# Layer 0's attention inputs projected with features on partitions, and queries and keys reloaded in thirds

## The chip, the cores and the metric

The kernel runs on one core of one Trainium2 chip. The metric is the device time of one execution in microseconds. The kernel before took 3854.85 us, the median of 3 runs (3852.91 to 3861.53).

## The reference

One step of a two-layer model: 128 context tokens and 1024 latent tokens (a grid 64 wide), 1152 tokens of 1024 features, fp32. The change concerns the attention of layer 0. Its input projection gives for every token queries, keys and values of 8 neighbourhood heads of 64 features and of 4 differential heads, whose queries and keys have two parts of 64 and whose values have 128:

```python
nq, nk, nv, dq, dk, dv = attn_projections(h_lat, w_in_attn[i])
dq, dk = axial_rope(dq), axial_rope(dk)          # per half of 32: [x1*cos - x2*sin, x1*sin + x2*cos]
o_na = neighbourhood_attention(nq, nk, nv, cache_na_k[:, i], cache_na_v[:, i], na_rpb[i])
k_all = jnp.concatenate([dk, cache_diff_k[:, i]], axis=1)
v_all = jnp.concatenate([dv, cache_diff_v[:, i]], axis=1)
o_df = diff_attention(dq, k_all, v_all, lam, lam_init)
mix_lat = jnp.concatenate([...o_na..., ...o_df...], axis=-1) @ w_out_attn[i]
```

The context tokens go through the same projections without rotation, and attend to themselves alone; their keys and values are outputs too. Differential attention takes two softmaxes (one of each part of queries and keys), subtracts lam times the second from the first, multiplies with the values and normalises. Neighbourhood attention lets a latent token see a window of 8 rows by 16 columns, with a bias, and the 128 cached tokens.

## The kernel before, in words

Products of fp32 numbers are made from a high and a low part (fp32r), three matmuls for one. Activations h and weights are split in that way, and for the scores the high and low parts of 64 features are stacked to 128 rows, so that two matmuls make one product.

*Projection.* `attn_in` (L355) with `proj_tok` (L332) works in 8 groups g: 0 to 3 are the differential heads, 4 to 7 pairs of neighbourhood heads. A group's weights are 8 blocks of 128 features by 384 columns (queries, keys, values, 128 each), loaded (L338) and split. For each of 9 tiles of 128 tokens, 24 matmuls with the tile's activations stationary and 384 weight columns streaming (L350 to L352) give tokens on partitions; ScalarE copies the result (L368, tile `ist`) and a write (L369) puts it into the DRAM tensor `qkv[g]`.

*Keys of a head.* `prep_k` (L408) loads them back in three pieces (L417 to L422, `kraw`). `stage` (L381) rotates the differential ones (VectorE L387 and L394, GpSimd L397) and splits them (ScalarE L403 or L405, VectorE L406). 20 turns on TensorE by the identity (L429) put features on partitions, and ScalarE copies them into the tile `K` (L434, L437).

*Queries.* For each of a head's 9 units (a unit is a head and 128 query tokens) `prep_q` (L440) does the same with one tile (`qraw`, L504 or L617; the neighbourhood gather L617 takes 8 x 16 rows of the grid): 4 turns (L446) and a cast into `Q` by VectorE (L448).

*Units.* `pipe` (L567) runs units with lags of their steps between them: preparing `Q`, scores (L518, L519; L636, L645), exponentials (L524), turning the probabilities (L476) and multiplying with the values (L482). Between the steps `fill` pulls background work: in stage A, the differential heads, 0.28 of a projection step of the later groups and 0.3 of a step of the adaptive vectors (`aw` loads L128, sums L181); in stage B, the neighbourhood heads, the output projection (weights `owraw`, L744, one buffer; attention results `xr`, L699 and L702). Stage B also loads the biases (`nab`, L624, two for each unit) and values (`vw`, on GpSimd's queue).

*Order.* The source gives the steps, and a scheduler with a timeline of its own sets the order of the instructions on each engine and on SP, the queue that issues nearly all loads and writes. Tiles of one tag share a small number of buffers (`ist` 2, `qraw` 2, `kraw` 2, `K` 2, `Q` 3, `aw` 2), and an instruction that needs a buffer waits for its last readers. An engine, and SP, works in its order.

Of the kernel before, what the change touches and what calls it, by code (L numbers as in the profile page):

```python
# [40 lines left out]

SHARED = ("K", "Q", "pT", "qraw", "kraw", "st2", "st3", "mx", "sm")


class Net:
# [286 lines left out]
    def proj_tok(self, hH, hL, wsrc, ncol, pool, sink):  # L332

        nc = self.nc
        WH, WL = [], []
        for k in range(KT):
            raw = self.t(pool, [P, ncol], tag="wraw")
            nc.sync.dma_start(raw if ncol != GW else raw.rearrange("p (m c) -> p m c", c=P), wsrc(k))  # L338
            wh = self.t(pool, [P, ncol], F32R, tag="wh")
            wl = self.t(pool, [P, ncol], F32R, tag="wl")  # L340
            self.split(wh, wl, raw)
            WH.append(wh)
            WL.append(wl)
        yield
        for T in range(NT):
            pt = self.t(self.nps, [P, 512], tag="mm")
            c = slice(T * P, (T + 1) * P)
            for k in range(KT):
                mm = nc.tensor.matmul
                mm(pt[:, :ncol], lhsT=hH[k][:, c], rhs=WH[k], start=k == 0, stop=False)  # L350
                mm(pt[:, :ncol], lhsT=hH[k][:, c], rhs=WL[k], start=False, stop=False)  # L351
                mm(pt[:, :ncol], lhsT=hL[k][:, c], rhs=WH[k], start=False, stop=k == KT - 1)  # L352
            sink(T, pt)
            yield


    def attn_in(self, g, hH, hL, pool):
        nc, I, O = self.nc, self.I, self.O
        j = g if g < 4 else g - 4
        blk = 3 if g < 4 else 0  # L360
        w = I["w_in_attn"][0]

        def wsrc(k):
            return w[k * P : (k + 1) * P, :].rearrange("p (m c) -> p m c", c=512)[:, blk : blk + 3, j * P : (j + 1) * P]

        def sink(T, pt):
            st = self.t(pool, [P, GW], tag="ist")
            nc.scalar.copy(st, pt[:, :GW])  # L368
            nc.sync.dma_start(self.qkv[g][T * P : (T + 1) * P, :], st)  # L369
            if T == 0:  # L370
                if g < 4:
                    nc.scalar.dma_start(O[4][0, 0, :, j].rearrange("t c d -> t (c d)"), st[:, P : 2 * P])
                    nc.scalar.dma_start(O[5][0, 0, :, j], st[:, 2 * P :])
                else:
                    nc.scalar.dma_start(O[2][0, 0, :, 2 * j : 2 * j + 2].rearrange("t c d -> t (c d)"), st[:, P : 2 * P])
                    nc.scalar.dma_start(O[3][0, 0, :, 2 * j : 2 * j + 2].rearrange("t c d -> t (c d)"), st[:, 2 * P :])

        return self.proj_tok(hH, hL, wsrc, GW, pool, sink)

    def stage(self, p, raw, n, slots, scale, rope):  # L380

        nc = self.nc
        if rope is not None:
            cs, sn = rope
            m1 = self.t(p, [P, n, P], tag="rm1", bufs=1)
            m2 = self.t(p, [P, n, P], tag="rm2", bufs=1)
            nc.vector.tensor_tensor(  # L387
                m1.rearrange("p n (c d) -> p n c d", d=64),
                raw.rearrange("p n (c d) -> p n c d", d=64),
                cs.unsqueeze(2).to_broadcast([P, n, 2, 64]),  # L390
                op=ALU.mult,
            )
            sw = raw.rearrange("p n (h x q) -> p (n h) x q", x=2, q=16)[:, :, ::-1, :]
            nc.vector.tensor_tensor(  # L394
                m2.rearrange("p n (h x q) -> p (n h) x q", x=2, q=16), sw, sn.rearrange("p n (h x q) -> p (n h) x q", x=2, q=16), op=ALU.mult
            )
            nc.gpsimd.tensor_tensor(m1, m1, m2, op=ALU.add)  # L397
# [8 lines left out]
        nc.vector.scalar_tensor_tensor(st[:, :, 1, :], rv, scale, st[:, :, 0, :], op0=ALU.mult, op1=ALU.subtract)  # L406
        return st.rearrange("p a b c -> p a (b c)").bitcast(F32)

    def prep_k(self, g, cache, rope, p, ps):
        nc = self.nc  # L410
        K = self.t(p, [P, 2, 10 * P], F32R, tag="K")
        src = self.qkv[g]
        for tiles in ((0, 9), (1, 2, 3, 4), (5, 6, 7, 8)):
            n = len(tiles)
            raw = self.t(p, [P, n, P], tag="kraw")
            if tiles[0] == 0:
                nc.sync.dma_start(raw[:, 0, :], src[0:P, P : 2 * P])  # L417
                nc.sync.dma_start(raw[:, 1, :], cache)
# [1846 lines left out]
```

## Time and profile before

| | us |
|---|---|
| median of 3 runs | 3854.85 (3852.91 to 3861.53) |
| the profiled execution | 3851.15 |
| its span, first to last instruction | 3849.4 |
| stage A, projections and differential heads | 108 to 600 |
| boundary | 600 to 640 |
| stage B, neighbourhood heads | 640 to 911 |

The stage marks were read from the timeline. The rest of the span (layer 0's feed-forward, layer 1 and the normalisations) uses none of the changed functions. How to read the views: a group's row gives line, engine, operation, tile names (out<-in), shape and count, then busy us, mean ns of one, and the idle time just before, with what ended it. A window's row gives start and end, length, busy us (and instructions) of TensorE (PE), its weight loads (PEld), VectorE (DVE), ScalarE (ACT) and GpSimd (POOL), TensorE's granted clock, the mean busy share of the 16 DMA engines, and GB/s. A row of SP's timeline gives the start and length of the issue of a DMA, not of its transfer.

### The profile page before, as it was taken

How to read it: one execution, taken by the hardware profiler on the slowest of the kernel's cores; microseconds unless marked ns; L12 is line 12 of the kernel's file. 1: busy time of each engine (PE TensorE's matmuls, PEld its weight loads, DVE VectorE, ACT ScalarE, POOL GpSimd, SP SyncE). 2: the span in 40 equal slices, each digit the busy share in tenths (PEclk: the TensorE clock that was granted, in tenths of full speed). 3: DMA queues.
4: the chain of work that ended last, by engine and by line, in shares of the span. 5: the costliest groups of instructions: out<-in, count | busy, mean ns of one | idle time of the engine just before them, and what ended most of it. 6: DMA issues, size and time to landing. Idle time of an engine off the chain costs nothing.

```text
span 3849.4 us, 67037 instructions
## 1 busy us (share of the span) xinstructions
PE 3661.5 (95%) x24885; PEld 3444.4 (89%) x24885; DVE 2272.7 (59%) x5106; ACT 1404.6 (36%) x3361; POOL 1100.4 (29%) x1450
## 2 busy tenths in 40 slices
PE   7999997999999999999999998999998999999998
PEld 4899996999899999999989886877777899999998
DVE  6677864665945556665244556766665774444434
ACT  3445444555333333225332333233322533334221
POOL 2000002112222224333011323665662322324430
PEclk9999997999999999999999998999999999999999
DMA  6433325542223334442334336232223212223321
GB/s 209 125 94 107 113 69 133 133 109 61 64 85 108 91 99 143 149 137 86 106 105 130 115 129 212 58 88 65 65 60 108 62 60 75 75 73 107 116 88 61
DMA packets 425399, 392.16 MB, mean 102 GB/s; under 512 B 68172, under 2 KB 370376, under 8 KB 423536
## 3 DMA queue, kind: packets, MB, share of 16 engines
q1 hardware_dynamic: 406640, 376.29, 32.3%
q10 hardware_dynamic: 13152, 7.27, 0.7%
q0 software_dynamic: 5280, 4.31, 0.6%
q8 instruction: 197, 3.23, 0.3%
q14 instruction: 130, 1.06, 0.1%
HBM read 289.32 MB, written 98.33 MB: 101 GB/s over the span
## 4 chain that ended last, share of the span: by engine, by line
PE 74%; DVE 8%; DMA 8%; POOL 3%; issue 2%; ACT 2%; SPq 0%; DVEq 0%; ACTq 0%; POOLq 0%
PE mm L82 8%; PE mm L84 8%; PE mm L83 8%; PE A L1726 3%; PE A L1724 3%; PE A L1725 3%; PE o L482 3%; DMA aw<-in_w_ada_dram 2%; PE E L1724 2%; PE E L1725 2%; PE mm L350 2%; PE E L1726 2%; PE mm L352 2%; PE mm L351 2%; DVE aacc L181 2%
## 5 line engine op out<-in xcount | busy, mean ns | idle before, releaser
L729 DVE SCALAR_TENSOR_TENSOR x<-mm,mod,x 128x128 f32<-128x128 f32 (+1 forms) x576 | 277.2, 512 | 238.7 <-PE mm L84 237.9
L1636 POOL TENSOR_TENSOR wl<-raw,wh 128x512 fp32r<-128x512 f32 x120 | 167.1, 1392 | 567.2 <-ACT wh L1635 541.3
L1635 ACT CAST wh<-raw 128x512 fp32r<-128x512 f32 x288 | 178.3, 620 | 306.4 <-PE A L1725 107.4
L181 DVE SCALAR_TENSOR_TENSOR aacc<-aw,v,aacc 128x512 f32<-128x512 f32 x280 | 228.7, 849 | 75.2 <-DMA aw<-in_w_ada_dram 74.7
L350 PE MATMUL mm<-wh,hH 128*128 128x384 f32 x576 | 200.8, 349 | 11.5 <-ACT wh L74 4.7
L352 PE MATMUL mm<-wh,hL 128*128 128x384 f32 x576 | 195.8, 341 | 4.6 <-DVE hL L261 4.6
L351 PE MATMUL mm<-wl,hH 128*128 128x384 f32 x576 | 197.3, 342 | 1.0 <-DVE wl L75 0.9
L82 PE MATMUL mm<-hH,wh 128*128 128x384 f32 x528 | 184.6, 351 | 2.6 <-ACT wh L74 2.6
L84 PE MATMUL mm<-hH,wl 128*128 128x384 f32 x528 | 180.3, 344 | 3.4 <-DVE rst L867 2.1
L83 PE MATMUL mm<-hL,wh 128*128 128x384 f32 x528 | 180.3, 342 | 0.0
L1636 DVE TENSOR_TENSOR wl<-raw,wh 128x512 fp32r<-128x512 f32 x168 | 118.8, 708 | 102.1 <-ACT wh L1635 98.3
L397 POOL TENSOR_TENSOR rm<-rm,rm 128x128 f32<-128x128 f32 (+1 forms) x40 | 27.0, 676 | 461.2 <-DVE rm L387 329.0
L75 DVE TENSOR_TENSOR wl<-wraw,wh 128x256 fp32r<-128x256 f32 (+1 forms) x184 | 90.1, 508 | 108.3 <-ACT wh L74 78.7
L1150 PE MATMUL A<-AR,BK 64*128 64x256 f32 x576 | 116.8, 418 | 31.3 <-DVE KK L1154 18.6
L524 ACT ACTIVATE P<-S,mx 128x384 f32<-128x384 f32 (+1 forms) x200 | 112.2, 570 | 88.8 <-DVE mx L522 86.6
L82 PE MATMUL mm<-mh,owh 128*128 128x384 f32 x384 | 138.5, 375 | 5.2 <-ACT owh L74 2.7
L83 PE MATMUL mm<-ml,owh 128*128 128x384 f32 x384 | 132.5, 345 | 0.0
L84 PE MATMUL mm<-mh,owl 128*128 128x384 f32 x384 | 131.3, 342 | 1.2 <-DVE owl L75 1.2
L350 PEld LDWEIGHTS mm<-wh,hH 128*128 128x128 f32 x576 | 110.2, 191 | 16.2 <-ACT ist L368 7.7
L817 PE MATMUL mm<-wh,hH 128*128 128x256 f32 x432 | 124.0, 290 | 0.0
L1150 PEld LDWEIGHTS A<-AR,BK 64*128 64x128 f32 x576 | 75.4, 194 | 53.1 <-issue 20.0
L818 PE MATMUL mm<-wl,hH 128*128 128x256 f32 x432 | 122.4, 285 | 0.0
(540 smaller groups left out, 12501.5 us busy)
## 6 DMA issues: line engine op xcount, KB each, us to landing
raw<-in_w_ffn_in_dram SPq DMA_DIRECT2D x176, 256.0 KB
aw<-in_w_ada_dram SPq DMA_DIRECT2D x160, 256.0 KB
raw<-hdr SPq DMA_DIRECT2D x132, 192.0 KB
hdr<-c SPq DMA_DIRECT2D x160, 144.0 KB
raw<-in_w_ffn_out_dram SPq DMA_DIRECT2D x88, 256.0 KB
F<-stg SPq DMA_DIRECT2D x34, 640.0 KB
stg<-st SPq DMA_DIRECT2D x12, 1536.0 KB
qkv<-ist SPq DMA_DIRECT2D x72, 192.0 KB
```

What stands on the lines that cost most here:

```text
L82: mm(out, lhsT=wh, rhs=xh, start=first, stop=False)
L83: mm(out, lhsT=wh, rhs=xl, start=False, stop=False)
L84: mm(out, lhsT=wl, rhs=xh, start=False, stop=last)
L181: nc.vector.scalar_tensor_tensor(acc[:, c, :], w[:, 0, :], s, acc[:, c, :], op0=ALU.mult, op1=ALU.add)
L350: mm(pt[:, :ncol], lhsT=hH[k][:, c], rhs=WH[k], start=k == 0, stop=False)
L351: mm(pt[:, :ncol], lhsT=hH[k][:, c], rhs=WL[k], start=False, stop=False)
L352: mm(pt[:, :ncol], lhsT=hL[k][:, c], rhs=WH[k], start=False, stop=k == KT - 1)
L729: self.nc.vector.scalar_tensor_tensor(x[f][:, c], pt[:, a:b], self.mod[l][jg][:, f, cd : cd + 1], x[f][:, c], op0=ALU.mult, op1=ALU.add)
L1636: eng.tensor_tensor(wl, w, wh, op=ALU.subtract)
L1724: mm(o, lhsT=wh[:, ks], rhs=xh, start=new and k == 0, stop=False, skip_group_check=True)
L1725: mm(o, lhsT=wh[:, ks], rhs=xl, start=False, stop=False, skip_group_check=True)
L1726: mm(o, lhsT=wl[:, ks], rhs=xh, start=False, stop=k == 3, skip_group_check=True)
```

## The change

The projection takes the three parts of a group one after the other: keys, values, queries. Now a block of 128 weight columns is stationary and 384 tokens stream (`mm3`, L82 to L84): 9 steps of 24 matmuls as before, but the result has features on partitions. Keys and queries go to DRAM as `qf[g][m]`, 128 features x 1152 tokens. The differential heads' go a second time, as `qs[g][m]`, with neighbouring blocks of 16 features exchanged (8 writes of 16 rows), which is the partner that the rotation needs. Values are turned back to tokens on partitions by 3 turns for each third (L358), go to `vt[g]`. The context's keys for the output take one turn. Neighbourhood queries are written patch by patch, so that a unit's 128 tokens are together.

`heads_steps` prepares a head in 13 steps: the cached keys (2 turns, as they come by tokens), 6 pieces of keys and 6 of queries. A piece (`fm_piece`) is 64 features of one part by 384 tokens, loaded twice, onto partitions 0 to 63 and 64 to 127, by one DMA whose source pattern is 2 x 64 x 384, with a step of 0 in the 2 (`fraw`; in the built program the pattern is the same). For the rotation, the same pattern of `qs` (`fsw`), two products and a sum. Then ScalarE casts the high part for all rows, and VectorE subtracts: for keys on the lower 64 rows alone, for queries into a second tile. The units use slices of `K` and `Q`, with no turn. Steps of a head are pulled by `heads_hook` at the start of its units, and the first 9 of the next head's during the last four units; so the first neighbourhood head's begin in stage A. `ist` has 3 buffers, `fraw` 2, `fsw` 2.

SP at the start of the first head (group 0 just projected; `kraw` keys, `qraw` queries, `wraw` the next group's weights). Before:

```order
L417 DMA kraw_884<-qkv_107 128x128
L418 DMA kraw_884<-in_cache_diff_k_dram 128x128
L369 DMA qkv_107<-ist_768 128x384
L504 DMA qraw_946<-qkv_107 128x128
L504 DMA qraw_1048<-qkv_107 128x128
L369 DMA qkv_107<-ist_796 128x384
L422 DMA kraw_897<-qkv_107 128x4x128
L504 DMA qraw_1156<-qkv_107 128x128
L369 DMA qkv_107<-ist_824 128x384
L369 DMA qkv_107<-ist_852 128x384
L338 DMA wraw_990<-in_w_in_attn_dram 128x3x128
```
And now:

```order
L435 DMA kraw_981<-in_cache_diff_k_dram 128x128
L418 DMA fraw_990<-qf_108 128x1x384
L422 DMA fsw_992<-qs_124 128x1x256
L364 DMA vt_131<-ist_859 128x3x128
L418 DMA fraw_999<-qf_108 128x1x384
L422 DMA fsw_1001<-qs_124 128x1x256
L435 DMA kraw_1804<-in_cache_diff_k_dram 128x128
L422 DMA fsw_1010<-qs_124 128x1x384
L382 DMA qf_107<-ist_887 128x384
L386 DMA qs_123<-ist_887 16x384 x8
L364 DMA vt_131<-ist_902 128x3x128
L382 DMA qf_107<-ist_930 128x384
```
Loads of `qkv` tiles among the last writes of group 0 became pieces of keys, in a swapped and an unswapped copy; the writes of the queries and of their swapped copies (`qs_123`, eight each) stand behind the first of them, and the next weights further on.

TensorE in the middle of stage A, between projection matmuls (`T` a turn's result, `S` scores). Before:

```order
L351 MATMUL mm_1425<-wl_1005,hH_28_132 128x384
L476 MATMUL T_1260<-ident_60,P_1179 128x128 x4
L446 MATMUL T_1306<-ident_60,st_269_1302 128x128 x4
L352 MATMUL mm_1425<-wh_1004,hL_36_140 128x384
L350 MATMUL mm_1425<-wh_1010,hH_29_133 128x384
L351 MATMUL mm_1425<-wl_1011,hH_29_133 128x384
L352 MATMUL mm_1425<-wh_1010,hL_37_141 128x384
L518 MATMUL S_1390<-K_883,Q_1172 128x384
```
And now, at a like place:

```order
L83 MATMUL mm_1462<-hL_37_165,wh_1116 128x384
L84 MATMUL mm_1462<-hH_29_157,wl_1117 128x384
L502 MATMUL T_1385<-ident_60,P_1295 128x128 x4
L358 MATMUL T_1419<-ident_60,ist_1340 128x128 x3
L539 MATMUL S_1510<-K_980,Q_1044 128x384
L540 MATMUL S_1510<-K_980,Q_1044 128x384
```
The four turns of queries (L446) are gone; three turns of values by L358 stand at some of these places, and the scores' stationary operand is a slice of a query tile made for three units.

SP at the boundary between the stages (`owraw` output-projection weights, `xr` attention results and inputs, `nab` biases). Before:

```order
L702 DMA xr_7007<-in_x_sample_dram 128x3x128
L744 DMA owraw_7832<-in_w_out_attn_dram 128x1024
L744 DMA owraw_7939<-in_w_out_attn_dram 128x1024
L744 DMA owraw_8987<-in_w_out_attn_dram 128x1024
L744 DMA owraw_9111<-in_w_out_attn_dram 128x1024
L744 DMA owraw_10297<-in_w_out_attn_dram 128x1024
L624 DMA nab_1556_6878<-rpbd 128x1x384
L624 DMA nab_1557_6879<-rpbd 128x1x384
L624 DMA nab_1558_6880<-rpbd 128x1x384
L417 DMA kraw_7636<-qkv_112 128x128
L418 DMA kraw_7636<-in_cache_na_k_dram 128x128
L422 DMA kraw_7649<-qkv_112 128x4x128
```
And now:

```order
L761 DMA owraw_7730<-in_w_out_attn_dram 128x1024
L761 DMA owraw_7828<-in_w_out_attn_dram 128x1024
L418 DMA fraw_7272<-qf_118 128x1x384
L418 DMA fraw_7354<-qf_118 128x1x384
L761 DMA owraw_8769<-in_w_out_attn_dram 128x1024
L716 DMA xr_7025<-in_x_prompt_dram 128x128
L719 DMA xr_7025<-in_x_sample_dram 128x2x128
L418 DMA fraw_7358<-qf_118 128x1x384
L418 DMA fraw_7433<-qf_118 128x1x384
L761 DMA owraw_8875<-in_w_out_attn_dram 128x1024
L418 DMA fraw_7437<-qf_118 128x1x384
L418 DMA fraw_7519<-qf_118 128x1x384
```
The loads of output-projection weights, in a row before, have key pieces of the second pair of neighbourhood heads (`qf_118`) between them, and the first biases stand further on.

The diff, cut to its core:

```diff
     def attn_in(self, g, hH, hL, pool):
...
+        def turn(st, tg, n, dst):
+            pt = self.t(self.nps, [P, 512], tag="T")
+            for i in range(n):
+                nc.tensor.transpose(pt[:, i * P : (i + 1) * P], st[:, i * P : (i + 1) * P], self.ident)
+            o = self.t(pool, [P, GW], tag="ist")[:, : n * P]
+            nc.scalar.copy(o, pt[:, : n * P])
...
+        for m in (1, 2, 0):
+            ms = slice(m * P, (m + 1) * P)
+            for tg in range(TG):
+                sl = slice(tg * GW, (tg + 1) * GW)
+                pt = self.t(self.nps, [P, 512], tag="mm")
+                for k in range(KT):
+                    self.mm3(pt[:, :GW], WH[k][:, ms], WL[k][:, ms], hH[k][:, sl], hL[k][:, sl], k == 0, k == KT - 1)
+                st = self.t(pool, [P, GW], tag="ist")
...
+                        nc.sync.dma_start(self.qf[g][m][:, sl], st)
+                        if g < 4:
+                            for b in range(8):
+                                o = (b ^ 1) * 16
+                                nc.sync.dma_start(self.qs[g][m][o : o + 16, sl], st[b * 16 : b * 16 + 16])
...
+    def fm_piece(self, p, g, m, c, a, n, rope):
+        nc = self.nc
+        dup = lambda src, a, n: dap(src, 64 * c * TOK + a, [[0, 2], [TOK, 64], [1, n]])
+        raw = self.t(p, [P, GW], tag="fraw")[:, :n]
+        nc.sync.dma_start(raw, dup(self.qf[g][m], a, n))
+        if rope:
+            l0 = max(a, P) - a
+            sw = self.t(p, [P, GW], tag="fsw")[:, : n - l0]
+            nc.sync.dma_start(sw, dup(self.qs[g][m], a + l0, n - l0))
+            ts = slice(a + l0 - P, a + n - P)
+            nc.vector.tensor_tensor(sw, sw, self.sin[:, ts], op=ALU.mult)
+            nc.vector.tensor_tensor(raw[:, l0:], raw[:, l0:], self.cos[:, ts], op=ALU.mult)
+            nc.gpsimd.tensor_tensor(raw[:, l0:], raw[:, l0:], sw, op=ALU.add)
+        return raw
+
+    def heads_steps(self, g, cache, rope, scale, p, ps, head):
...
+        for tg in range(TG):
+            for c in range(2):
+                a = tg * GW
+                r = self.fm_piece(p, g, 1, c, a, GW, rope)
+                o = K[:, c, a : a + GW]
+                nc.scalar.copy(o, r)
+                nc.vector.tensor_tensor(o[64:], r[64:], o[64:], op=ALU.subtract)
+                yield
+        for tg in range(TG):
+            Q = head["Q", tg] = self.t(p, [P, 2, 2, GW], F32R, tag="Q")
+            for c in range(2):
+                r = self.fm_piece(p, g, 0, c, tg * GW, GW, rope)
+                nc.scalar.activation(Q[:, c, 0, :], r, AF.Copy, scale=scale)
+                nc.vector.scalar_tensor_tensor(Q[:, c, 1, :], r, scale, Q[:, c, 0, :], op0=ALU.mult, op1=ALU.subtract)
+                yield
+
+    def heads_hook(self, j, T, heads, gen):
...
+        upto(j, min(9 + T, 13))
+        if T >= 5 and j < 7:
+            upto(j + 1, (2, 4, 6, 9)[T - 5])
...
-            K, Q = head[j][0], st["Q"]
+            K, Q = head[j]["K"], head[j]["Q", T // 3][:, :, :, T % 3 * P : T % 3 * P + P]
...
-                nc.tensor.matmul(S[:, :ch], lhsT=Q[:, 2 * c, :], rhs=kk, start=True, stop=False)
+                nc.tensor.matmul(S[:, :ch], lhsT=Q[:, c, 0, :], rhs=kk, start=True, stop=False)
...
-                self.wpool = _Bufs(wp, {"wraw": 3, "wh": 9, "wl": 9, "ist": 2, "aw": 2})
+                self.wpool = _Bufs(wp, {"wraw": 3, "wh": 9, "wl": 9, "ist": 3, "aw": 2})
```

More of the change, by code (lines that the diff above doesn't have):

```diff
@@ L39, in dap @@
     return bass.AP(tensor=ap.tensor, offset=ap.offset + offset, ap=dims)
-SHARED = ("K", "Q", "pT", "qraw", "kraw", "st2", "st3", "mx", "sm")
+SHARED = ("K", "Q", "pT", "fraw", "kraw", "st", "mx", "sm")
 class Net:
@@ new lines, in heads_steps @@
+    def heads_steps(self, g, cache, rope, scale, p, ps, head):
+        nc = self.nc
+        K = head["K"] = self.t(p, [P, 2, 10 * P], F32R, tag="K")
+        raw = self.t(p, [P, P], tag="kraw")
+        nc.sync.dma_start(raw, cache)
+        st = self.t(p, [P, 2, 2, 64], F32R, tag="st")
+        rv = raw.rearrange("p (c d) -> p c d", d=64)
+        nc.scalar.copy(st[:, :, 0, :], rv)
+        nc.vector.tensor_tensor(st[:, :, 1, :], rv, st[:, :, 0, :], op=ALU.subtract)
+        sf = st.rearrange("p a b c -> p a (b c)").bitcast(F32)
+        yield
@@ L443, in prep_q @@
         pt = self.t(ps, [P, 512], tag="T")
         for c in range(2):
-            for s in range(2):
-                nc.tensor.transpose(pt[:, (c * 2 + s) * P : (c * 2 + s + 1) * P], st[:, c, s * 64 : s * 64 + P], self.ident)
-        Q = self.t(p, [P, 4, P], F32R, tag="Q")
-        nc.vector.tensor_copy(Q.rearrange("p a b -> p (a b)"), pt)
-        return Q
+            nc.tensor.transpose(pt[:, c * P : (c + 1) * P], sf[:, c, :], self.ident)
+        nc.scalar.copy(K[:, :, 9 * P :], pt[:, : 2 * P].rearrange("p (c t) -> p c t", c=2))
@@ L451, in diff_lam, with upto @@
+    def heads_hook(self, j, T, heads, gen):
+        def upto(j, k):
+            if j not in heads:
+                heads[j] = {"n": 0}
+                heads[j]["gen"] = gen(j, heads[j])
+            while heads[j]["n"] < k:
+                heads[j]["n"] += 1
+                next(heads[j]["gen"], None)
+        upto(j, min(9 + T, 13))
+        if T >= 5 and j < 7:
+            upto(j + 1, (2, 4, 6, 9)[T - 5])
     def diff_lam(self):
@@ L502, in a @@
         def a():
-            raw = self.t(p, [P, 1, P], tag="qraw")
-            nc.sync.dma_start(raw[:, 0, :], self.qkv[j][T * P : (T + 1) * P, 0:P])
-            st["Q"] = self.prep_q(p, ps, raw, None if T == 0 else (self.cos[:, T - 1 : T, :], self.sin[:, T - 1 : T, :]))
+            if T == 0:
+                head[j]["ob"] = self.t(p, [P, NT, P], tag="ob"), self.t(p, [P, NT], tag="oss", bufs=2)
         nk, k0, ch = (1, 0, P) if T == 0 else (9, P, GW)
@@ L1979, in attn @@
         wpool = self.wpool
+        done = set()
         def group(g):
-            return self.attn_in(g, hH, hL, wpool)
+            yield from self.first if g == 0 else self.attn_in(g, hH, hL, wpool)
+            done.add(g)
         due = {}
```

254 lines of the change are left out of this document (102 added, 152 removed).

## The prediction

> **What bounds the kernel now.** I read the page first: which engine is busiest, and what ends last.
>
> ```profile
> span 3849.4 us, 67037 instructions
> PE 3661.5 (95%) x24885; PEld 3444.4 (89%) x24885; DVE 2272.7 (59%) x5106; ACT 1404.6 (36%) x3361; POOL 1100.4 (29%) x1450
> PE 74%; DVE 8%; DMA 8%; POOL 3%; issue 2%; ACT 2%; SPq 0%; DVEq 0%; ACTq 0%; POOLq 0%
> ```
>
> TensorE (PE) is busy 95% of the span and holds 74% of the chain that ended last. But the change touches only layer 0's attention, so the next view is the busy time of each engine in its stages (start and end, length, busy us of PE, weight loads, DVE, ACT, POOL, granted clock, mean busy share of the 16 DMA engines, GB/s).
>
> ```profile
> 108.00:600.00 492.00, 476.69 (x3084) 463.30 (x3083) 362.44 (x902) 232.46 (x742) 25.74 (x39) 0.99 0.33 99
> 600.00:640.00 40.00, 20.12 (x102) 16.85 (x101) 20.33 (x51) 16.12 (x44) 11.21 (x16) 0.71 0.61 148
> 640.00:911.00 271.00, 255.87 (x1806) 247.17 (x1805) 151.30 (x445) 139.64 (x356) 32.21 (x48) 0.92 0.47 121
> ```
>
> From 108 to 600 us run the projections and the differential heads (I call it stage A), from 640 to 911 the neighbourhood heads, and between them lies a boundary; I take 600 to 911 together as stage B. In A, PE is busy 477 of 492 us at a clock of 0.99: PE sets the time. The DMA engines look idle, 0.33 and 0.47, but that is a mean over 16 engines. The change is about transfers, so the question is how many engines each new transfer uses.
>
> **What the change removes on PE.** 160 turns of keys and 288 of queries go (L429, L446). In their place come 8 groups x 10 turns after the projection and 8 x 2 for the cached keys, 96. Net 352 fewer. The projections keep their count: 1728 matmuls of 384 columns on either side. The price of a turn:
>
> ```profile
> L446 PE MATMUL T<-ident,st 128*128 128x128 f32 x288 | 46.8, 288 | 1.7 <-ACT K L437 1.7
> L429 PE MATMUL T<-ident,st 128*128 128x128 f32 x160 | 24.5, 296 | 8.5 <-DVE st L406 8.5
> 125.20 0.33 PE L351 MATMUL mm<-wl,hH 128*128 128x384 f32 x1
> 125.37 0.34 PE L352 MATMUL mm<-wh,hL 128*128 128x384 f32 x1
> 125.55 0.60 PE L446 MATMUL T<-ident,st 128*128 128x128 f32 x4
> 125.91 0.42 PE L350 MATMUL mm<-wh,hH 128*128 128x384 f32 x1
> 126.17 0.33 PE L351 MATMUL mm<-wl,hH 128*128 128x384 f32 x1
> ```
>
> The mean of 288 ns contains overlap. The timeline gives the price: projection matmuls start 0.17 us apart (125.20, 125.37), with four turns between them 126.17 - 125.37 = 0.80 us pass for two matmuls and the turns. Less 2 x 0.174 that is 0.45, so 0.112 us a turn. 352 x 0.112 = **39.4 us** less on PE, wherever PE sets the time. The waits ahead of the turns, 8.5 + 1.7 us, go too: about 10.
>
> **Vector, scalar and GpSimd work.**
>
> ```profile
> L448 DVE CAST Q<-T 128x512 fp32r<-128x512 f32 x72 | 49.5, 687 | 16.3 <-PE T L446 15.6
> L387 DVE TENSOR_TENSOR rm<-kraw,cos 128x512 f32<-128x512 f32 x8 | 5.5, 690 | 3.2 <-DMA kraw<-qkv 2.9
> L397 POOL TENSOR_TENSOR rm<-rm,rm 128x512 f32<-128x512 f32 x8 | 11.7, 1463 | 150.2 <-DVE rm L387 49.4 <-DVE rm L394 35.7 <-DVE mx L522 25.9
> ```
>
> The new pieces put 192 operations of up to 384 columns on DVE; at no more than the 0.69 us of 512 columns that is 132 us, and the casts' 49.5 go at least: at most +83 on 534 busy of 803. POOL gets 48 additions, at most 48 x 1.463 = 70 us, and is busy 69 of 803. ACT swaps copies for copies. None becomes the bound: I take 0 on the path, cover: PE's 753 busy us. If an engine stops for a load, this cover is gone; that case is in the next part.
>
> **What the change adds on the queues.** 96 loads of 128x384 fp32 (196,608 bytes; "fraw") and 48 of the swapped copy ("fsw"; 32 of 384 columns, 16 of 256). All read 64 rows twice: the source pattern's outermost dimension is 2, the next 64. The trace holds no such load, so I look for what the outermost size does to others. First the issues on SP, then windows around their transfers.
>
> ```profile
> 207.97 0.32 SPq L369 DMA_DIRECT2D qkv<-ist  x1
> 748.69 1.25 SPq L624 DMA_DIRECT2D nab<-rpbd  x2
> 1536.79 0.33 SPq L1872 DMA_DIRECT2D raw<-hdr  x1
> 208.80:209.40 0.60, 0.60 (x6) 0.60 (x5) 0.58 (x1) 0.60 (x3) 0.00 (x0) 1.00 0.88 315
> 750.00:752.00 2.00, 2.00 (x17) 2.00 (x17) 1.58 (x5) 1.21 (x5) 0.00 (x0) 1.00 0.49 95
> 1538.20:1538.60 0.40, 0.40 (x4) 0.40 (x3) 0.40 (x2) 0.00 (x0) 0.00 (x0) 1.00 0.75 280
> 5.00:15.00 10.00, 3.33 (x15) 2.99 (x16) 4.86 (x13) 9.82 (x20) 0.00 (x0) 1.00 1.03 407
> nab<-rpbd SPq DMA_DIRECT2D x64, 192.0 KB
> qraw<-qkv SPq DMA_DIRECT2D x72, 64.0 KB
> kraw<-qkv SPq DMA_DIRECT2D x16, 256.0 KB
> SPq L369 <- ACT ist L368: 156.9, 45, 8.1
> ```
>
> One write of 128 rows (qkv) has 0.88 of the engines busy: 14 to 16 of them. But two bias loads in flight at once (nab, pattern 8 x 16 rows, outermost 8) hold the share at 0.49 for 2 us: eight engines, and the second load takes the same eight, else the share would be near 1. So I read that a load whose outermost size is 8 runs on 8 engines, always the same. By this a load with an outermost 2 runs on **two engines, and all 144 on the same two**.
>
> [...]
>
> The price: the aligned rows of 1536 bytes (raw<-hdr) move at 280 GB/s / (0.75 x 16) = 23.3 GB/s an engine; the best row has 407 / (1.03 x 16) = 24.7; the bias loads, whose rows start 4 bytes apart, have 95 / (0.49 x 16) = 12.1. The new rows are aligned and 1536 long, so I take 23.3 and keep 12.1 as the other bound. A long load then takes 196,608 / 2 / 23.3 = 4.22 us (8.1 at most), one of 256 columns 2.81 (5.4), however little else runs.
>
> SP itself: 144 loads, 56 writes of queries and keys, 192 small ones of 16 rows (qs) and 24 of values come, 168 DMAs go, net 248 at 0.32 us (qkv) to 0.62 (half of nab's 1.25), 79 to 154 us of issuing in 803. I take 0, near the lower end: SP has slack, it spent 157 us in A on waiting for ACT's copy of a projection (L369). If that slack is gone it is a part of the idle time below.
>
> **Stage A** holds 60 fraw (four heads, and the first neighbourhood head, now prepared early) and 48 fsw: 92 long and 16 short, 92 x 4.22 + 16 x 2.81 = 433 us on each of the two engines. Three long and two short (18) stand in SP's order ahead of the work that now starts at 108; 415 are left. The other traffic gives each engine its mean, 0.33 x 492 = 162 us; the qs writes that come (192 x 24,576 bytes, 4.7 MB) and the half of the query and key reads that goes from A (36 x 64 KB + 8 x 256 KB, 4.5 MB) cancel. Sum 577 us on two engines, against 492 now and against 477 - 39 that PE needs. So the pair becomes the bound: without any idle time A ends at 108 + 577 = 685, **+85**.
>
> It will idle. Each tag has two buffers, so at most four loads are in flight; SP is one queue, and behind a load that waits for its buffer stand the weight loads, the ada_vec loads (aw) and the writes of the projections; DVE works in order, so a multiplication that waits for its load holds the maxima and casts behind it, and PE the scores behind those. PE idles 803 - 753 = 50 us, 6%, of both stages under its own in-order feed. I take twice that, 1/8, for a chain with one more engine in it: 577 x 8/7 = 659, A ends at 767, **+167**. PE's gain of 39 falls into its idle time.
>
> **Stage B** has the other 36 fraw: 152 us. Other traffic 0.61 x 40 + 0.47 x 271 = 152. If the two are among the bias loads' eight, their real share there is above the mean by half of 64 loads x 196,608 / 8 / 12.1 = 2.03 us: +65. The old query gathers (36 x 64 KB on eight engines, 12.7 us at 23.3 GB/s) and key loads (8 x 256 KB on sixteen, 5.6) go: -18. Sum 351 against 311: +40; with 1/8 idle 402: **+91**. At the boundary PE idles half the time already:
>
> ```profile
> 615.14 1.97 PE L476 MATMUL T<-ident,P 128*128 128x128 f32 x8 [7.49 <-DVE P L541]
> 598.49 24.09 SPq L744 DMA_DIRECT2D owraw<-in_w_out_attn_dram  x5
> ```
>
> There five loads of out-projection weights hold SP for 24 us; the new order puts the fraw loads between them. The early preparation of the first neighbourhood head cannot save more than these 20 us of idle PE, and its loads have been counted in A.
>
> **The sum.** The profiled execution took 3851.15 us around its span of 3849.4, 3.7 under the median of 3854.85. Without idle 3851 + 85 + 40 = 3976; with it 3851 + 167 + 91 = **4109**. I forecast 4110. The ends: B hidden and A without idle 3851 + 85 = 3936; all at 12.1 GB/s: A 92 x 8.12 + 16 x 5.42 = 834, less 35, plus 162 = 961, +469; B 292 + 152 + 65 - 18 = 491, +180; together 4500.
>
> **The rivals.** *Spread loads (faster).* The loads use all 16 engines, or each its own pair, for instance because the 128 rows of the destination decide: then 108 loads add 92 x 196,608 / 16 / 23.3 = 0.53 us each, 49 us to 162, PE stays the bound and saves 39.4 and the 10 of the waits: 3851 - 49 = 3802. For it: writes with 128 rows reach 0.88. Against it: the bias loads have 128 rows in the destination too and stay at 0.49.
>
> *Hidden pair (no change).* Two engines carry the loads, but PE's work hides them. For A to keep its 492 us the pair's own 415 must fall to 492 - 162 = 330, a long load to 3.36 us, 29 GB/s an engine. For it: the rows above were measured beside other busy engines, and a pair alone may move more. Against it: no row has more than 24.7, and B would need its 351 to be 311. About 3850.
>
> *Slow rows (slower still).* Each row is written beside its double, and if an engine moves the two copies no faster than the bias rows, 12.1 GB/s, the sum is 4500. For it: the bias loads also read from a table in DRAM. Against it: their rows overlap and are unaligned, the new ones not.
>
> *Not what it says.* The doubled pattern could be merged into another shape when the program is built; there it still stands as 2 x 64 x 384, so this has no chance of its own beyond the first rival's.
>
> **Chances.** Pair at 23 GB/s, the sum above: 0.72. Slow rows 0.10. Spread 0.13. Hidden 0.05. The measurement tells about 0.2%, 7.7 us, from no change: faster 0.13 and a little of hidden, 0.14; same 0.03; slower 0.83. The likeliest case alone goes from 3936 to some 4300 (idle up to a quarter: 577 x 4/3 = 769, ends at 877, +277; 351 x 4/3 = 468, +157; 4285). The range 3900 to 4500 takes in the slow rows and leaves out spread and hidden, 0.18.
>
> **What would show it.** Stretches of several us in stages A and B with a DMA share near 2/16 = 0.12 while PE and DVE wait for fraw and fsw; stage A's end, now 600, at 685 or later; PE's granted clock in A below 0.99, as at the boundary (0.71). A fraw load alone should move some 47 GB/s. If A ends at 600 or sooner with shares near 1 under the loads, the step from 8 to 2 is wrong. If the long stretches at 0.12 are there and A ends on time, the idle share and the place of the loads are wrong. Idle PE behind DVE with the pair unused would make the two buffers, not the engines, the cause.

## The result

The changed kernel takes 4243.7 us (median of 4 runs, 4240.03 to 4252.91), the kernel before beside it 3855.24; the ratio is 1.1008, with a 95% interval of 1.0986 to 1.1031. It is slower by 10%, as forecast in sign; the forecast was 4110 with a range of 3900 to 4500. The profiled execution has a span of 4244.0 us, 394.6 more than before.

The page of the changed kernel, busy time of the engines and the chain that ended last:

```profile
span 4244.0 us, 66548 instructions
PE 3754.2 (88%) x24533; PEld 3516.4 (83%) x24533; DVE 2275.1 (54%) x5058; ACT 1397.5 (33%) x3293; POOL 1119.1 (26%) x1458
PE 56%; DMA 9%; DVE 7%; POOL 4%; issue 3%; ACT 1%; SPq 0%; DVEq 0%; ACTq 0%; POOLq 0%
```

TensorE has 352 matmuls fewer (24,533 for 24,885) and is yet busy for 93 us more. Its clock is lower (0.922 for 0.971 on the mean of the span, and by stages in the next views): a matmul of 128 x 384 by L82 takes 368 ns on the mean, where L350 and L82 took 349 and 351. The views cut the two kernels at the same events: the first scores of the four differential heads, the last of these, and the first and last scores of latent tokens in the neighbourhood heads (start and end, length, busy us of PE, PEld, DVE, ACT, POOL, granted clock, DMA share, GB/s). Before:

```profile
61.00:126.90 65.90, 56.68 (x315) 54.79 (x314) 37.44 (x74) 20.41 (x44) 10.61 (x10) 0.95 0.45 129
126.90:253.30 126.40, 119.61 (x749) 114.23 (x750) 91.64 (x222) 58.16 (x185) 7.62 (x10) 0.97 0.33 98
253.30:374.70 121.40, 120.58 (x799) 118.34 (x797) 95.94 (x236) 57.87 (x191) 6.68 (x10) 1.00 0.35 103
374.70:497.60 122.90, 121.25 (x792) 118.73 (x791) 97.15 (x243) 61.03 (x194) 6.46 (x11) 0.99 0.37 109
497.60:606.90 109.30, 102.96 (x680) 100.37 (x679) 75.03 (x196) 50.59 (x166) 3.23 (x7) 0.98 0.24 71
606.90:640.80 33.90, 16.85 (x78) 14.17 (x76) 16.25 (x44) 13.11 (x34) 11.21 (x16) 0.64 0.66 159
640.80:878.60 237.80, 224.62 (x1611) 218.81 (x1610) 140.51 (x416) 127.69 (x330) 32.21 (x48) 0.93 0.49 126
```

And after the change:

```profile
61.00:184.70 123.70, 61.36 (x285) 56.39 (x284) 41.70 (x82) 19.48 (x42) 14.67 (x14) 0.71 0.30 92
184.70:394.60 209.90, 138.46 (x704) 130.66 (x705) 93.14 (x214) 56.24 (x172) 16.79 (x17) 0.77 0.26 81
394.60:592.50 197.90, 137.56 (x735) 129.37 (x734) 102.18 (x237) 60.13 (x187) 14.74 (x12) 0.82 0.31 94
592.50:783.20 190.70, 139.28 (x780) 134.09 (x780) 102.86 (x243) 62.12 (x192) 11.04 (x12) 0.83 0.31 91
783.20:916.60 133.40, 112.47 (x675) 108.04 (x675) 70.89 (x186) 56.42 (x178) 0.00 (x0) 0.90 0.25 73
916.00:961.00 45.00, 18.52 (x91) 15.84 (x92) 18.19 (x48) 15.87 (x42) 10.81 (x16) 0.65 0.45 126
961.00:1259.00 298.00, 236.25 (x1395) 229.32 (x1393) 123.33 (x374) 112.58 (x264) 32.10 (x48) 0.78 0.40 110
```

By stages: +58 until the first scores, +84, +77 and +68 in the first three heads, +24 in the fourth (which loads no rotated pieces of a next head), so +310 at the last differential scores; +11 at the boundary, +60 in the neighbourhood heads; 14 come after the last of their scores, and have no known cause. In the first three heads PE is busy for 66 to 73% of the time, at a clock of 0.77 to 0.83 instead of 0.97 to 1.00. No other engine took its place: DVE is busy half of the time, and the DMA engines have a mean share of 0.26 to 0.31, less than before.

What everything waits for is seen in a stretch of 19 us in the first head: its window, SP, and the instructions of DVE that work on loaded pieces (a row ends with the idle time before it and what ended that).

```profile
215.00:234.00 19.00, 12.49 (x54) 12.17 (x54) 5.51 (x14) 3.33 (x9) 2.00 (x2) 0.77 0.13 47
216.45 17.43 SPq L422 DMA_DIRECT2D fsw<-qs  x3
219.66 0.56 DVE L425 TENSOR_TENSOR fraw<-fraw,cos 128x384 f32<-128x384 f32 x1 [3.28 <-DMA fraw<-qf]
223.66 0.56 DVE L424 TENSOR_TENSOR fsw<-fsw,sin 128x384 f32<-128x384 f32 x1 [3.45 <-DMA fsw<-qs]
227.67 0.56 DVE L425 TENSOR_TENSOR fraw<-fraw,cos 128x384 f32<-128x384 f32 x1 [3.39 <-DMA fraw<-qf]
231.68 0.56 DVE L424 TENSOR_TENSOR fsw<-fsw,sin 128x384 f32<-128x384 f32 x1 [3.38 <-DMA fsw<-qs]
```

The share is 0.13, which is 2.1 of 16 engines, at 47 GB/s. A load lands every 4.0 us, one after another; each product follows its load at once. If two engines halve a load, 98,304 bytes each in 4.0 us are 24.5 GB/s. Meanwhile the issue of three loads of fsw takes SP 17 us, and the projections' writes and weights stand behind. The waits from 61 to 970 us that a DMA ended (engine, instruction, what it waited for: us in total, times, longest):

```profile
DVE fraw L425 <- DMA fraw<-qf: 167.1, 48, 15.0
DVE fsw L424 <- DMA fsw<-qs: 133.5, 47, 6.7
ACT wh L74 <- DMA wraw<-in_w_in_attn_dram: 80.2, 16, 23.9
```

The same waits before, in the same window:

```profile
DVE rm L387 <- DMA kraw<-qkv: 2.9, 2, 2.1
ACT wh L74 <- DMA wraw<-in_w_in_attn_dram: 25.3, 22, 3.1
```

Before, no load of queries or keys kept DVE more than 2.9 us in all; here it is 300 us, and ACT waits 80 us instead of 25 for the projections' weights.

### The profile page after: what moved, and what is told of

It reads as the page before. It is cut to its first block, busy times and chain, and to the rows that moved or that the text cites. A ratio compares the mean times of both kernels' runs of the same rounds, so it can differ in the third digit from the quotient of the medians.

```text
span 4244.0 us, 66548 instructions
## 1 busy us (share of the span) xinstructions
PE 3754.2 (88%) x24533; PEld 3516.4 (83%) x24533; DVE 2275.1 (54%) x5058; ACT 1397.5 (33%) x3293; POOL 1119.1 (26%) x1458
## 4 chain that ended last, share of the span: by engine, by line
PE 56%; DMA 9%; DVE 7%; POOL 4%; issue 3%; ACT 1%; SPq 0%; DVEq 0%; ACTq 0%; POOLq 0%
PE mm L82 8%; PE mm L84 8%; PE mm L83 8%; PE A L1743 3%; PE A L1741 3%; PE A L1742 3%; DMA fraw<-qf 2%; PE E L1741 2%; PE E L1742 2%; PE E L1743 2%; DMA aw<-in_w_ada_dram 2%; DMA F<-stg 2%; PE o L508 1%; POOL MB L1218 1%; POOL tf L1217 1%
## 5 line engine op out<-in xcount | busy, mean ns | idle before, releaser
L82 PE MATMUL mm<-hH,wh 128*128 128x384 f32 x1104 | 405.4, 368 | 103.8 <-ACT wh L74 45.0
L84 PE MATMUL mm<-hH,wl 128*128 128x384 f32 x1104 | 394.3, 358 | 15.9 <-DVE wl L75 12.8
L83 PE MATMUL mm<-hL,wh 128*128 128x384 f32 x1104 | 394.5, 358 | 7.5 <-DVE hL L261 7.5
L82 PEld LDWEIGHTS mm<-hH,wh 128*128 128x128 f32 x1104 | 225.1, 204 | 120.5 <-ACT wh L74 47.0
L84 PEld LDWEIGHTS mm<-hH,wl 128*128 128x128 f32 x1104 | 223.3, 202 | 24.6 <-DVE wl L75 17.0
L83 PEld LDWEIGHTS mm<-hL,wh 128*128 128x128 f32 x1104 | 225.4, 204 | 10.7 <-DVE hL L261 7.8
L508 PE MATMUL o<-V,pT 128*128 128x128 f32 x584 | 94.6, 306 | 63.6 <-ACT pT L504 21.8
L82 PE MATMUL mm<-mh,owh 128*128 128x384 f32 x384 | 143.7, 389 | 3.5 <-ACT mh L74 2.3
L508 PEld LDWEIGHTS o<-V,pT 128*128 128x128 f32 x584 | 86.3, 216 | 69.9 <-ACT pT L504 24.0
L502 PE MATMUL T<-ident,P 128*128 128x128 f32 x556 | 102.7, 310 | 45.2 <-ACT pT L504 22.6
L539 PE MATMUL S<-K,Q 128*128 128x384 f32 (+1 forms) x200 | 83.2, 418 | 61.4 <-ACT P L545 55.2
```

The source lines that it names most:

```text
L82: mm(out, lhsT=wh, rhs=xh, start=first, stop=False)
L83: mm(out, lhsT=wh, rhs=xl, start=False, stop=False)
L84: mm(out, lhsT=wl, rhs=xh, start=False, stop=last)
L508: nc.tensor.matmul(o, lhsT=pT[:, i * P : (i + 1) * P], rhs=vs(b + i), start=b + i == 0, stop=b + i == nk - 1)
```

## Experiments

The theory: the pattern's outermost size sets how many DMA engines a load uses, here two, and loads that take eight times as long set the time. The rivals: it is the step of 0 or the one big DMA; it is the chain of load, DVE, GpSimd and ACT with two buffers; it is SP's queue with 192 small writes. All ratios are to the kernel before on the same chip. The edits are shown against the changed kernel (those of e2 and e7 against e1, those of e11 and e12 against the kernel before).

**e1: the doubled loads as two plain ones.**

```diff
+        half = lambda src, a, n: dap(src, 64 * c * TOK + a, [[TOK, 64], [1, n]])
+        def twice(dst, src, a, n):
+            for d in range(2):
+                nc.sync.dma_start(dst[64 * d : 64 * d + 64], half(src, a, n))
...
-        nc.sync.dma_start(raw, dup(self.qf[g][m], a, n))
+        twice(raw, self.qf[g][m], a, n)
...
-            nc.sync.dma_start(sw, dup(self.qs[g][m], a + l0, n - l0))
+            twice(sw, self.qs[g][m], a + l0, n - l0)
```

> The change with one edit: each doubled load (source 2 x 64 x 384 with a step of 0) is issued as two DMAs of 64 plain rows, one for each half of the partitions. Same bytes, same buffers, more issues on SP (144 more). Theory (a load with an outermost 2 runs on two engines, and these two set the time): each of the two now spreads, a load takes some 0.5 us of every engine instead of 4.2 us of two, the loss is gone and the gain of the turns shows: 3800 us (3785 to 3830), faster than before; the first scores, at 185 us in the changed kernel and 127 before, return to about 130. Rival (the loss comes from the in-order chain load, DVE, GpSimd, ACT with two buffers, or from SP's queue with 192 small writes more, whatever the number of engines): it stays above 4050, or grows with the 144 issues.

Measured: 3903.82 us, ratio 1.0147 (1.0117 to 1.0177). It is 340 us below the changed kernel, which was 389 above before, with the same buffers and more issues, so neither the buffers nor SP carry the bulk. That the loads spread is seen in a window in which SP issues only such loads and three of weights:

```profile
130.00:145.00 15.00, 3.25 (x6) 1.58 (x6) 9.45 (x16) 3.36 (x7) 4.89 (x5) 0.50 0.50 142
```

The share is 0.50 and 142 GB/s move, three to four times what the change had. But 3800 was expected, and 57 us are left on the slow side (the kernel before took 3846.83 on this chip). The theory holds for the bulk; the credit for the turns does not show.

**e2 and e7: two DMAs as in e1, but on two and on four engines.** Only the order in which the source's rows are taken differs from e1; e7 has 4, `4 * TOK` and 16 where e2 has 2, `2 * TOK` and 32:

```diff
-        half = lambda src, a, n: dap(src, 64 * c * TOK + a, [[TOK, 64], [1, n]])
+        half = lambda src, a, n: dap(src, 64 * c * TOK + a, [[TOK, 2], [2 * TOK, 32], [1, n]])
```

> As e1, two DMAs of 64 rows for each doubled load, but the source's rows are taken even ones first, then odd ones: pattern 2 x 32 x 384, no step of 0. The rows land in a permuted order, so queries and keys have their features mixed and the output is not the reference's; the work and the bytes are those of e1. Theory (the outermost size of the pattern sets the number of engines, always the same): two engines again, each load 64 x 1536 bytes on each as in the changed kernel, 4240 us (4180 to 4330). Rival (it was the step of 0, the reading of the same row twice, or one DMA with 128 rows instead of two): like e1, near 3800.

> As e2, but the rows taken in steps of four (pattern 4 x 16 x 384): by the theory four engines, each load half as long as in e2; output not the reference's for the same reason as in e2. It tells how the cost goes with the time that a load takes. Capacity (sum of each engine against TensorE's): four engines have 208 us of their own in stage A and some 160 of others, hidden: as e1, 3900 (3885 to 3930). Cost with the time of each load that is waited for (e2 less e1: 309 us at 4.2 us a half-pair of loads on two engines, against 0.5 on sixteen): half of the time keeps somewhat under half of the 309, 4040 (3990 to 4080).

Measured: e2 4213.13 us, 1.0959 (1.0921 to 1.0996); e7 3989.72, 1.0375 (1.0340 to 1.0409). A stretch of each, e2 first, in which SP issues almost nothing but such loads:

```profile
447.20:461.20 14.00, 7.30 (x36) 6.50 (x34) 2.36 (x6) 3.63 (x11) 2.37 (x2) 0.88 0.13 48
```

```profile
133.60:143.00 9.40, 1.70 (x3) 0.79 (x3) 4.45 (x7) 1.53 (x3) 1.89 (x3) 0.50 0.27 96
```

0.13 and 48 GB/s, 0.27 and 96: by the share 2.1 and 4.3 of 16 engines, so two and four. There is no step of 0 and no DMA of 128 rows in e2, and it is as slow as the change but for 30 us. Between e1, e2 and e7 only the order of the rows differs, so at these sizes, 64, 2 and 4, it is the outermost one that decides; the rival falls. Over e1 two engines cost 309 us and four 86. Neither of the two readings in the expectation of e7 gives that: it is more than nothing, and at the lowest end of what the second allowed (3990). Halving the time of a load (96 for 48 GB/s in these stretches) took away almost three quarters of its cost. VectorE's waits for these loads, from 61 to 970 us, go the same way: 301 us in the change, 249 in e2, 105 in e7, 50 in e1.

**e3 and e4: only one kind of load split.** e3 has the second replacement of e1 (fsw), e4 the first (fraw).

> Only the swapped copies' loads (48, all in stage A) are split in two as in e1; the 96 loads fraw stay doubled. It tells how the cost adds up. Theory A (capacity: the two engines' sum against TensorE's): stage A has 60 long loads left, 253 us and some 162 of other traffic, below the 440 that TensorE needs, so A's loss of 320 goes but for a late start (some 30); stage B keeps its 36 loads and its loss (75): about 3930 (3880 to 3990). Theory B (each doubled load is waited for in order, so cost goes with their number): 60 of 108 loads keep 178 of 320 us in A, and B 75: about 4100.

> Only the 96 loads fraw are split in two; the 48 of the swapped copies stay doubled, on two engines. Stage B has none then. Theory A (capacity): A's two engines have 32 x 4.22 + 16 x 2.81 = 180 us of their own and 162 of others, hidden: about 3840 (3800 to 3870). Theory B (cost with the number of loads that are waited for): 48 of 108 loads keep 142 of 320 us, less TensorE's 49: about 3950.

Measured: e3 4120.6 us, 1.0710 (1.0684 to 1.0736); e4 3990.35, 1.0371 (1.0334 to 1.0407). Splitting fsw takes 123 us from the change, splitting fraw 253, together 376 where both at once take 340. So the cost goes rather with the number of slow loads (theory B: 4100 and 3950, too low by 21 and 40), and not with the two engines' sum against TensorE's (theory A: 3930 and 3840). Per us of their transfer on the pair, at the forecast's price (180 for fsw, 96 x 4.22 = 405 for fraw), it is 0.68 and 0.62 us.

**e5 and e6: the swapped copies' writes on GpSimd's queue, and left out.**

```diff
-                                nc.sync.dma_start(self.qs[g][m][o : o + 16, sl], st[b * 16 : b * 16 + 16])
+                                nc.gpsimd.dma_start(self.qs[g][m][o : o + 16, sl], st[b * 16 : b * 16 + 16])
```

e6 has no such line, and `twice(sw, self.qf[g][m], ...)`.

> e1, and the 192 small writes of the swapped copies (16 rows each) are issued on GpSimd's queue instead of SP's. In e1 SP issues DMAs back to back from 100 to 160 us, eight of these writes take it 3.7 us, 24 x 3.7 = 88 us in all, and TensorE waits for the next group's weights behind them (14.4 us at 119, 5.9 at 135, 4.9 at 143). Theory (what is left of the loss in e1, 57 us above before, and the 40 to 50 of gain that do not show, is SP's issuing): 3903 falls to 3840 (3815 to 3865). Rival (it is the lower granted clock and DVE's longer waits, or GpSimd's own order becomes late: 192 issues of some 0.7 us ahead of its additions): within 15 us of e1, or above.

> e1 without the 192 writes of the swapped copies at all; the loads fsw read the unswapped queries and keys instead, so the rotation is wrong and the output is not the reference's. Everything else is as in e1. It is the bound of what these writes cost. Theory (SP's issuing): 3820 (3795 to 3850), below e5 if GpSimd's queue costs something, equal if not. Rival (the writes' place on SP does not matter): 3890 or more.

Measured: e5 3912.25 us, 1.0168 (1.0145 to 1.0192); e6 3878.56, 1.0083 (1.0051 to 1.0115). Moving the writes does not help; without them e1's 1.0147 becomes 1.0083, some 25 us. They come from the start. There e1 has (SP's timeline, then PE's):

```profile
113.17 3.68 SPq L386 DMA_DIRECT2D qs<-ist  x8
117.91 3.67 SPq L386 DMA_DIRECT2D qs<-ist  x8
122.10 3.66 SPq L386 DMA_DIRECT2D qs<-ist  x8
```

```profile
133.46 0.69 PE L82 MATMUL mm<-hH,wh 128*128 128x384 f32 x1 [14.35 <-ACT wh L74]
```

Three times eight writes hold SP for 11 us, the first weights of the next group are issued behind them and six loads of pieces at 130 us, and PE stands for 14 us. In e6 the first scores are at 128 us, in e1 at 149, before at 127. So the place on SP mattered at the first head, by 20 us, and little later. In e5 the first scores come at 163, though PE has done more by then (busy 73.9 us from 61 us on, 49.9 in e1). GpSimd's queue is not seen to be the reason: its last such writes end at 150, and it stands idle for 12 us before the addition at 162. Why e5 gains nothing stays open. The expectation of 3840 and 3820 missed: 26 us above before stay in e6, though it has none of these writes.

**e9 and e10: a third buffer for fraw**, in e1 and in the change.

```diff
-        bp = _Bufs(both.enter_context(self.pool("kAB")), {"K": 2, "Q": 3, "pT": 2, "fraw": 2})
+        bp = _Bufs(both.enter_context(self.pool("kAB")), {"K": 2, "Q": 3, "pT": 2, "fraw": 3})
```

> e1 with a third buffer for the loads fraw (2 before; there is no room for more). If the loss that is left in e1 comes from pieces that wait for a buffer: 3904 falls by 15 or more, to 3885 or less. If it comes from SP's issuing and the start of the first head: within 10 us of e1.

> The change itself, doubled loads on two engines, with a third buffer for the loads fraw. The prediction had the two engines idle 1/8 of the time because of the two buffers; in the changed kernel they idle more. If the buffers are what keeps them idle, the third shortens stage A and the kernel by 40 us or more, to 4200 or less. If the idle time comes from the order (pieces bunched at the ends of the heads, queries that wait for their tile Q, weights queued behind them): 4244 within 25.

Measured: e9 3899.67 us, 1.0120 (1.0075 to 1.0164), beside e1's 1.0147; e10 4239.29, 1.1009 (1.0968 to 1.1051), beside 1.1008. The buffers of fraw are not what is short, in either. No run has a third for fsw beside it. In the change SP waits for fsw's buffers, which an addition on GpSimd frees (from 61 to 1305 us):

```profile
SPq L422 <- POOL fraw L426: 88.9, 25, 11.0
```

In e10 the same wait is 41.1 us and the time is the same, which speaks against these buffers as well; a run of their own is missing.

**e8: the neighbourhood half alone.** Groups 0 to 3 take the old path, 4 to 7 the new one with split loads (the edit's core; the old functions return with it, and some tiles lie in other pools):

```diff
-            yield from self.first if g == 0 else self.attn_in(g, hH, hL, wpool)
+            yield from self.first if g == 0 else (self.attn_in_tok if g < 4 else self.attn_in)(g, hH, hL, wpool)
```

> Only the neighbourhood half of the change, with its loads split in two as in e1: groups 4 to 7 are projected with features on partitions and reloaded by thirds, groups 0 to 3 and the differential heads are as before (qkv tiles, turns on TensorE, rotation by tokens), and the first neighbourhood head is prepared in stage B, not ahead. No rotation, so no swapped copies and none of the 192 small writes. It takes 216 of 448 turns away and adds 48, net 168 x 0.112 = 19 us of TensorE. Theory (the differential half costs, by the swapped copies on SP at the start and its waits in the heads, 22 us at the start and 31 in the heads in e1; the neighbourhood half gains a little, 11 us in e1 for the boundary and stage B): 3840 (3828 to 3852), faster than before by up to 0.6%. Rival (the loads' latency costs stage B as much as the turns gave): 3852 to 3875.

Measured: 3891.1 us, 1.0102 (1.0069 to 1.0134). Slower, not 3840, and above the rival's 3875 as well: this half costs too. Its windows at the boundary and in stage B, and PE's longest wait between 600 and 960 us:

```profile
600.00:640.00 40.00, 30.41 (x200) 28.45 (x198) 22.57 (x57) 19.82 (x62) 7.29 (x11) 0.94 0.42 119
640.00:911.00 271.00, 221.09 (x1466) 212.44 (x1466) 137.89 (x413) 127.85 (x300) 35.79 (x54) 0.88 0.60 141
```

```profile
PE T L852 <- DMA xr<-in_x_sample_dram: 23.3, 5, 15.9
```

The last differential scores come at 623 us instead of 607, the last neighbourhood scores at 904 instead of 879. In stage B the DMA share is 0.60 where it was 0.47, and PE waits 23 us for input tiles in the queue among the pieces, where before such waits were 3.6. So this half's pieces and its projections cost more than 168 turns gave; which of the two weighs more is not told apart. Why e1, which contains this half, is level with before at the boundary and in stage B (below) is not settled; e1 prepares the first pair ahead, in stage A, and its tiles lie in other pools.

**e12: 56 slow loads that nobody reads, in the kernel before.**

```diff
+            for _ in range(1 + T % 2 if T else 2):
+                d = self.t(self.dmp, [P, GW], tag="dm", bufs=2)
+                nc.gpsimd.tensor_copy(d[:, 0:2], r1)
+                nc.sync.dma_start(d, dap(self.I["w_ffn_in"][0], 0, [[0, 2], [TOK, 64], [1, GW]]))
```

> Not the change: the kernel before, with 56 loads added to stage A, one or two for each differential unit, each 2 x 64 x 384 with a step of 0 like fraw (196,608 bytes), into a tile that nothing reads. A copy of two numbers on GpSimd ahead of each ties it to its unit. So two engines get 56 x 4.22 = 236 us more, besides 162 of other traffic in 492 us, and no instruction waits for the data, but what stands behind it on SP and on these two engines may. Theory (the loss of the change comes from work that waits for slow loads in order): 3860 (3850 to 3880), the 56 issues cost a little. Rival 1 (loads of others that queue behind on the two engines, weights and aw, carry the loss): 3920 or more. Rival 2 (capacity alone, sums of two engines): also hidden, 3852 to 3860; told apart from the theory by e3 and e4, which the sums did not explain.

Measured: 3913.45 us, 1.0164 (1.0142 to 1.0186), 60 us. Its waits from 61 to 680 us:

```profile
ACT wh L74 <- DMA wraw<-in_w_in_attn_dram: 55.8, 19, 7.3
DVE aacc L181 <- DMA aw<-in_w_ada_dram: 30.4, 13, 7.0
SPq L546 <- POOL dm L545: 86.8, 37, 7.3
```

Before, the first two were 25.3 and 6.5 us (61 to 640). What made them longer, no view here shows. The time is outside the theory's range (3850 to 3880) and close to the first rival's 3920, so the theory as I put it, that only waits for the slow loads themselves cost, is not borne out: others wait as well. But SP also stood for 87 us for the copies that pace the loads, which can delay the same weights; how much of the 60 is due to either is not settled.

**e11: the same finding applied to the kernel before.** Its three patterns with an outermost 8 are turned round:

```diff
-                nc.sync.dma_start(raw[:, 0, :], dap(src, (P + rh * 512 + w * 16) * GW, [[64 * GW, 8], [GW, 16], [1, P]]))
+                nc.sync.dma_start(raw[:, 0, :], dap(src, (P + rh * 512 + w * 16) * GW, [[GW, 16], [64 * GW, 8], [1, P]]))
...
-                    nc.sync.dma_start(nb[:, P:], dap(self.rpbd, off, [[RPB_ROW, 8], [1, 16], [1, GW]]))
+                    nc.sync.dma_start(nb[:, P:], dap(self.rpbd, off, [[1, 16], [RPB_ROW, 8], [1, GW]]))
...
-                nc.sync.dma_start(dap(od, (P + rh * 512 + w * 16) * P, [[64 * P, 8], [P, 16], [1, P]]), ost)
+                nc.sync.dma_start(dap(od, (P + rh * 512 + w * 16) * P, [[P, 16], [64 * P, 8], [1, P]]), ost)
...
+    sel[:] = np.ascontiguousarray(sel.transpose(0, 1, 3, 2)).reshape(sel.shape)
```

> Not the change: the kernel before, with the same finding applied to its own patterns. The bias loads (nab), the neighbourhood queries' gathers (qraw) and the outputs' writes (odr) have 8 x 16 rows, outermost 8; here the two dimensions are exchanged (16 x 8), the tokens of a unit stand in the other order everywhere, and the table that selects the mask is exchanged with them. The result is the reference's. Theory (the outermost size sets the engines): windows in which two bias loads are in flight show a share near 1 where before had 0.49, a load takes half as long; the time gains only what stage B waits for these loads (6.8 us of VectorE's waits before): 3845 (3835 to 3853). Rival (the size does not matter here): the share stays 0.49 and the time 3852.

Measured: 3841.02 us against 3852.89, ratio 0.9972 (0.9957 to 0.9986): 0.3% below the kernel before, little, but beyond the interval. The neighbourhood scores of its profiled execution, first to last:

```profile
640.30:872.80 232.50, 220.82 (x1613) 214.71 (x1612) 139.74 (x417) 127.40 (x330) 32.16 (x48) 0.95 0.59 130
711.50:713.50 2.00, 2.00 (x17) 1.95 (x16) 1.96 (x8) 2.00 (x8) 2.00 (x4) 1.00 1.15 234
```

232.5 us instead of 237.8, and VectorE's waits for nab fall from 6.8 to 2.2 us. The share goes beyond the old 0.49 with two bias loads in flight, though input loads run beside them in that window, so it is no clean count of engines. The span of this one execution is 3849.3 us, as before; the gain stands on the medians.

## Why the prediction was right, and where not

*Two engines, always the same.* Right: the stretches at 0.13, the clock below 0.99 and the end of A behind 685 us are those that the prediction named, and e1, e2 and e7 part the cause from its rivals. The step from eight engines to two was an estimate from one pattern's share, 0.49; the runs have 0.13 with an outermost 2 (the change, e2) and 0.27 with 4 (e7). That it is the same two each time is read from the first head: loads issued at 212.97, 213.53 and 214.95 us are in flight together, and yet the share stays at 0.13 and they land 4.0 us apart.

*The price, 4.22 us (23.3 GB/s).* 4.0 us in the changed kernel, 24.5 GB/s. The slow rows, 12.1 GB/s, don't apply.

*Stage A, +167.* The step that failed is the term "with 1/8 idle". The pair's 577 us of work were to end at 767; A's last scores came 310 us later than before, not 167, so by the forecast's own 577, over the 809 us from 108 to 917, the pair was busy for 71% and idle for 29% (an estimate; no view gives the two engines alone). The reason given, two buffers and in-order engines fed by them, is in part wrong: a third fraw buffer changes nothing (e10); fsw's buffers were not tested. What the runs show in its place is a cost for each slow load, of about 0.6 us for each us of transfer on two engines (e3, e4), but of 86 / 292 = 0.3 on four (e7; 292 is half of 405 + 180). It stays where the pair's sum falls below TensorE's (e3: 253 + 162 against some 440). In the changed kernel the readers stop one after another (DVE 300 us), SP stands behind them, the weights come late (ACT 80 us), and PE's clock is lower in the heads with the pauses (0.77 to 0.83). A sum of a resource's work against the bound's work, with a flat idle share, is not a model of this.

*Stage B and the boundary, +91.* 11 + 60 = 71 until the last scores and 14 behind them, 85. The number is near, but no run shows that the pair set the time there, or that its two engines are among the eight of the bias loads, on which the +65 rests. In e1 these two stages are 11 us shorter than before, so the slow loads cost about 82 us for the 152 of their transfer, 0.54 per us, much as in stage A; that 1/8 idle gave nearly the same is luck as far as is known. The result lies within the likeliest case (up to 4285) because its two parts missed to opposite sides: stage A went beyond its end (+310 against +277), stage B stayed far below (+85 against +157).

*TensorE's 39 us.* The turns went, the time did not show in any kernel here. In e1 the same seven stages are, by length: 87.7, 125.3, 144.3, 130.6, 110.9, 26.7 and 233.8 us. Its sum against before, with the busy time of PE (the sums of the two answers):

```profile
sum 859.30, PE 747.92 PEld 717.26 DVE 553.99 ACT 382.28 POOL 102.59; mean PE 106.85 PEld 102.47 DVE 79.14 ACT 54.61 POOL 14.66
```

```profile
sum 817.60, PE 762.56 PEld 739.44 DVE 553.96 ACT 388.87 POOL 78.03; mean PE 108.94 PEld 105.63 DVE 79.14 ACT 55.55 POOL 11.15
```

PE has 15 us less of busy time, not 39, at a lower clock in the first two heads (0.91 and 0.94 for 0.97 and 1.00), and 859 - 748 = 111 us idle instead of 55. The loss is +22 at the start, +31 in the heads, -7 at the boundary, -4 in stage B, and some 10 us behind the last scores. The start is SP's writes (e6). The heads' part stays open: a delay half as large, 16 us, is there in e8 too, where the heads are as before and mainly the projections of groups 4 to 7 differ; no run isolates the cause of either.

*SP at 0.* Wrong at the first head, where SP has no slack: 20 to 25 us (e6). Averaged over 803 us the slack was there; at the point where the first head and the next weights compete it was not.

*Vector, scalar and GpSimd at 0.* DVE is busy as long as before (554 us in both sums above), so they did not become the bound.

*The rivals.* Hidden and slow rows are out. The spread rival's mechanism is e1, and its price, 3802, was 100 us too good, by the last three points. Had the loads spread, I should have forecast faster and been wrong.

## What to carry to other kernels

Give a DMA's pattern a large outermost size: the same rows moved at 142 GB/s with 64 (e1, three loads of weights among them), at 96 with 4 (e7) and at 48 with 2 (e2), and 16 instead of 8 took 0.3% off the kernel before (e11). Two copies as two DMAs cost two issues, 1.1 to 1.3 us of SP in e1 for 0.5 in the change, and one DMA with a leading 2 ran on two engines (a share of 0.13, 4.0 us for 192 KB). Where a load feeds an in-order chain, price the wait for it at each place and what queues behind, not only the sum of its resource: halving the loads' time took almost three quarters of the cost (e7 against e2), and a third buffer of fraw nothing (e10). Work saved on the busiest engine is worth nothing as long as its inputs come later by more (e1: 15 us less of work, 56 us more idle), and small writes that are cheap on average can hold the queue at the one place where weights must pass (24 writes, 11 us of SP in e1).

## What the hardware showed that I had not expected

Loads that nobody reads cost time as well: 56 of them 60 us in a kernel whose DMA engines had a mean share of 0.33 in stage A before (e12; how much of it comes from the copies that pace them is open). And issuing 192 small writes from GpSimd was no better than from SP (1.0168 against 1.0147), although GpSimd was busy for only 45 of the 511 us of e1's heads.
